# A decoder layer on one Trainium2 core: the last 6 feature blocks of the down projection as 7 products of quarters, placed at the end

## The chip, the core and the metric

The kernel runs on one core of a Trainium2 chip. The core has engines with instruction streams of their own: PE (TensorE, matrix products, with PEld for its weight loads), DVE (VectorE), ACT (ScalarE), POOL (GpSimd) and SP (SyncE, which here only issues transfers). They meet through semaphores. Transfers run on 16 DMA engines; SP, ACT and POOL issue them, and those that add to what lies at their destination are issued by POOL, on a software queue. The metric is the device time of one execution in microseconds: 1019.4 us, the median of three runs (1019.25 to 1019.58).

## The reference, cut to what matters

One layer (`DEPTH = 1`) on x of 512 positions by 1024 features, float32: a gated mixer of three branches, a residual sum, and a gated ConvFFN; at the end an RMSNorm. The part at issue is the last lines:

```python
def conv_ffn(u, w_up, conv_w, conv_b, w_down):
    h = causal_dwconv(u @ w_up, conv_w, conv_b)
    a, v = h[..., :D_FF], h[..., D_FF:]
    return (jax.nn.silu(a) * v) @ w_down          # D_FF = 2816, to 1024 features
...
        x = x + conv_ffn(rmsnorm(x, ln2_g[i]), ...)
    return rmsnorm(x, final_g)
```

## The kernel before

**Products.** Every float32 operand is split into a high and a low part (float32r): ACT casts the high part (`cast`, line 195, tile `wh` for weights), DVE subtracts it to get the low part (`lows`, line 217, tile `wl`; "the split" below), and `mm3` (line 230) issues high x high, high x low, low x high into one PSUM bank. So a product over n blocks of 128 features is 3n matmuls of 128x128 by 512 columns.

**Jobs.** The program is a list of `Job`s: a weight tile, and a body that issues the products with it. The loop at the end of `trunk` runs `prepare` and then the body of each: `prepare` of job n splits the weights of job n + 1 on DVE (and runs that job's `then`, if it has one), casts those of job n + 2 on ACT and fetches those of job n + 3 by SP (`fetch`, line 182) into one of two `raw` buffers. A job with `form` takes its weights from elsewhere than a fetch of its own, one with `load` set fetches nothing; one with `once` has the cast of job n + 2 issued whole in `prepare`, in two halves, otherwise a half at each `step`. `step()` is called between the products of a body and moves small sequences of other work on ("running"). PE, ACT, DVE and POOL execute their instructions in the order in which this program writes them down. A "read" below is DVE adding a finished bank to the residual `X1[tb, h]` (tb: 128 positions, four of them; h: half of the 1024 output features).

**The feed-forward part.** Of the 44 blocks of the up projection, 22 are gates and 22 values; `up_jobs` makes 22 jobs of two blocks. `up_evac` (line 1437) applies the convolution, and for a value block POOL multiplies it with its gate (line 1447); `later` then makes the operands of the down projection. The down projection runs over 22 feature blocks. The first 16 are two groups of 8 (`down_group`), each as 2x2 blocks of quarters in seven products in place of eight (the Strassen-Winograd scheme): positions are halved (`LO`, `HI`), features are halved into even and odd blocks, output features are halved. Their jobs are `one`, `five`, `three`, `six`, `seventh`, `two`, `four`, sums of the operands come from `sums_of` (four DVE operations of 256 columns, two casts, two splits for a pair of blocks), sums of weights from DVE (`diff`, line 343). The table `AT` says after which up job each of these jobs stands; the last two, `two` and `four`, stand after up job 21 and after the first job of the plain ending.

**The plain ending.** Blocks 16 to 21 go through `down_jobs(0)` and `down_jobs(1)`, one for each half of the output features: in each, a job of four blocks and one of two, and in them for each of the four tb a product over the blocks in their own operands (`ACTS`). In `down_jobs(1)` both jobs' products are held together (`tail=2`), so that it finishes one tb after another, 18 matmuls each. After the read of half 0 `early` (line 1586) takes the sum of squares and POOL multiplies by the gain (line 464); after the read of half 1 `norm_late` takes the other sum of squares on ACT (line 439), a square root on ACT (line 473), a reciprocal and its correction on DVE (lines 481 to 483), scales one half on DVE and one on ACT, and SP and ACT write both halves out (line 1605).

**A twin of the new ending.** The output projection of the mixer, `wo_group` (line 1266), is already a group of seven products over 8 blocks in the order `two, five, three, one, six, seven, four`, with a norm behind its last products (`first`, `then`), weight sums by adding transfers (`plus`, line 1288) and reads of two products replaced by a copy on ACT and an adding transfer of x (lines 1350 and 1351).

Of the kernel before, what the change touches and what calls it, by code (L numbers as in the profile page):

```python
# [10 lines left out]
F32 = mybir.dt.float32  # L11
# [5 lines left out]
P = 128  # L17
# [65 lines left out]
def trunk(ctx: ExitStack, tc, out, x, rel_bias, ln1_g, w_in, b_gate, w_a, pool_w, pool_scale, w_b,  # L83
# [22 lines left out]
    def T(name, dt=F32, shape=(P, S)):  # L106
        return big.tile(list(shape), dt, name=name, tag="t")
# [7 lines left out]
    def small(name, shape, dt=F32):  # L115
        return tiny.tile(list(shape), dt, name=name, tag="tiny")
# [110 lines left out]
    def wsrc(w, k0, k1, c0, c1):  # L227
        return w[k0 * P:k1 * P, c0:c1].rearrange("(k p) c -> p k c", p=P)
# [207 lines left out]
    def squares(eng, src, ss):  # L436
        junk = T("junk")
        if eng is act:
            act.activation(junk, src, AF.Square, accum_out=ss)
        else:  # L440
            dve.scalar_tensor_tensor(junk, src, 1.0, src, OP.mult, OP.mult, accum_out=ss)
# [14 lines left out]
            act.copy(hh, pv)  # L456
            dve.tensor_sub(ul[:, 4 * h:4 * h + 4, tb * P:(tb + 1) * P], pv, hh.bitcast(F32))

    def norm_early(t, g, h=0):

        ss, v0, xg = small("ss", [P, 1]), cpool.tile([P, 1], F32, name=f"v0_{len(V0)}"), T("xg")
        squares(act, t, ss)
        dve.tensor_scalar(v0, ss, 1.0 / D, EPS, OP.mult, OP.add)
        pool.tensor_tensor(xg, t, g[h], OP.mult)
        V0.append(v0)
        return v0, xg

    def norm_late(t, g, v0, outs, last, h=1, apart=False):


# [19 lines left out]
        (o1, x1), (o0, x0) = outs(xg)  # L490
        act.mul(o0, x0, rt)
        dve.tensor_scalar(o1, x1, rt, None, OP.mult)

    V0 = []

    uh = upool.tile([P, KD, S], F32R, name="uh", tag="uh")
    ul = upool.tile([P, KD, S], F32R, name="ul", tag="ul")
# [761 lines left out]
    def load_x1():  # L1259
        nxt["g2"] = grow(ln2_g[0])  # L1260
        act.activation(small("sq", [P, 1]), eps, AF.Sqrt)
        for tb, h in ((0, 1), (1, 1), (2, 0), (3, 0)):
            t = X1[tb, h] = T("x1")
            sp.dma_start(t, x[tb * P:(tb + 1) * P, h * S:(h + 1) * S])

    def wo_group():

        quarter = lambda two, h: w_o[:, h * S:(h + 1) * S].rearrange(
# [24 lines left out]

        def first(tb, h):
            half = 1 - h
            ss, xg = cpool.tile([P, 1], F32, name=f"so{tb}"), T("xg")
            squares(act, X1[tb, half], ss)
            pool.tensor_tensor(xg, X1[tb, half], nxt["g2"][half], OP.mult)
            nxt[tb] = ss, xg

        def then(tb, h):
            if "uh" not in nxt:
                nxt["uh"] = upool.tile([P, KD, S], F32R, name="uh2", tag="uh")
                nxt["ul"] = upool.tile([P, KD, S], F32R, name="ul2", tag="ul")
            ss, xg0 = nxt[tb]
            v0, vh = (cpool.tile([P, 1], F32, name=f"{n}{tb}") for n in ("va", "vo"))
            dve.tensor_scalar(v0, ss, 1.0 / D, EPS, OP.mult, OP.add)
            dve.tensor_scalar(vh, v0, -0.5, None, OP.mult)
            us = [T("u0"), T("u1")]
            it = norm_late(X1[tb, h], nxt["g2"], v0,  # L1310
                           lambda: (us[h], (us[1 - h], xg0)), vh, h, True)
            next(it)

            def rest(n=1):
                next(it, None)
                for _ in range(n):
                    yield
                norm_turn(us, nxt["uh"], nxt["ul"], tb)
# [118 lines left out]
    def up_evac(m, ps):  # L1437
        t = HC[m] = T("hc")
        act.activation(t, ps, AF.Identity, bias=ff["c1"][:, ff["b"] + m:ff["b"] + m + 1], scale=fw(2, m))  # L1439
        for k in range(2):  # L1440
            sh = 2 - k
            dve.scalar_tensor_tensor(t[:, sh:], ps[:, :S - sh], fw(k, m), t[:, sh:], OP.mult, OP.add)  # L1442
        if m < KF:
            act.activation(t, t, AF.Silu)  # L1444
            return
        a = HC[m - KF]
        pool.tensor_tensor(a, a, t, OP.mult)  # L1447

        def later():
            yield  # L1450
            k = m - KF
            if k >= KS or k % 2:
                h, l = T("fh", F32R), T("fl", F32R)
                act.copy(h, a)
                it = iter(())
                if k < KS:
                    it = sums_of(HC[k - 1], a, T("sah", F32R), T("sal", F32R),
                                 lambda j, h, l: FS.__setitem__((j, k // 2), (h, l)))
                    next(it)
# [123 lines left out]

    fin = {}

    def early(tb):
        yield
        v0, xg = norm_early(X1[tb, 0], fin["g"])
        vh = cpool.tile([P, 1], F32, name=f"vh{tb}")
        dve.tensor_scalar(vh, v0, -0.5, None, OP.mult)  # L1590
        fin[tb] = v0, vh, xg

    def down_jobs(h):

        def evac(tb, ps):
            t = X1[tb, h]
            dve.tensor_tensor(t, t, ps, OP.add)
            if h == 0:
                running.append(early(tb))
                return  # L1600
            v0, vh, xg0 = fin[tb]
            for _ in norm_late(t, fin["g"], v0, lambda xg1: ((xg1, xg1), (xg0, xg0)), vh):
                xg1 = _
            for i, o in ((1, xg1), (0, xg0)):
                (sp if i or tb < 3 else act).dma_start(out[tb * P:(tb + 1) * P, i * S:(i + 1) * S], o)

        return jobs_b(lambda k0, k1: [wsrc(w_down, KS + k0, KS + k1, h * S, h * S + S)], S,
                      lambda k, tb: ACTS[KS + k][0][:, tb * P:(tb + 1) * P],
                      lambda k, tb: ACTS[KS + k][1][:, tb * P:(tb + 1) * P], KF - KS, evac,
                      mk=(MM, SM)[h], tail=2 if h else 0)  # L1610


    class Call:
# [3 lines left out]
    def program():  # L1617
# [63 lines left out]
        between = {}  # L1681
        for group, ats in zip(groups, AT):
            for jobs_, at in zip(group, ats):
                between.setdefault(at, []).extend(jobs_)
        for i, job in enumerate(up_jobs()):
            yield job
            for load, ats in zip(loads, AT):
                if i == ats[0] - 3:
                    yield Call(load)
            yield from between.get(i, ())  # L1690
        yield Call(lambda: fin.setdefault("g", grow(final_g)))
        plain = down_jobs(0)
        yield next(plain)
        yield from between.get(2 * (KF // 2), ())
        yield from plain
        yield from down_jobs(1)

    jobs = list(program())
    weights = [j for j in jobs if isinstance(j, Job)]
# [216 lines left out]
```

## Time and profile before

| | |
|---|---|
| median of 3 runs | 1019.4 us |
| the profiled execution: its time | 1019.97 us |
| its span, first to last instruction | 1018.2 us |
| mean granted PE clock | 0.998 |
| DMA moved | 121.26 MB, mean 119 GB/s |
| software queue (POOL's transfers) | 2880 packets, 4.72 MB, 2.8% of the 16 engines' span |

In the rows below a timeline line reads: start in us from the span's start, duration in us, engine, source line, operation, tile written <- tiles read, shapes, count; in brackets the idle time before it on its engine and what released it. The chain of waits is followed back from the last instruction. Tiles: `pd` banks of the two groups, `pb` banks of the plain ending and of the output projection, `pu` of the up projection, `x` the residual, `wh`/`wl` high and low weights. The row of PE over a window gives us, PE busy (count), PEld, DVE, ACT and POOL busy, the clock, the DMA engines' share and GB/s.

### The profile page before, as it was taken

The page shows a single profiled execution, that of the slowest core. Times are in us where ns is not written, and L with a number is a line of the kernel's source. Part 1 is how long each engine was busy: PE and PEld are TensorE (multiplying, and loading weights), DVE is VectorE, ACT ScalarE, POOL GpSimd, SP SyncE. Part 2 cuts the span into 40 slices and gives each one's busy share as a digit, 9 for nine tenths or more (in the row PEclk, how much of TensorE's full clock was granted, in tenths as well). Part 3 has the DMA queues.
Part 4 walks back from the last instruction along what each step waited for, and adds up shares of the span by engine and source line. Part 5 has one row for each costly group of instructions (what it writes and reads, how often), then busy time and mean ns, then how long its engine had stood idle before and what let it go on. Part 6 is the DMA issues. An engine that isn't in the chain of part 4 may idle for free.

```text
span 1018.2 us, 13635 instructions
## 1 busy us (share of the span) xinstructions
PE 1005.1 (99%) x5378; PEld 856.6 (84%) x5378; DVE 718.1 (71%) x910; ACT 518.4 (51%) x878; POOL 147.7 (15%) x128
## 2 busy tenths in 40 slices
PE   8999999999999999999999999999999999999997
PEld 8898878999988888888888887898888888888885
DVE  6564768577767646676889688758778768685756
ACT  5433556454435565878567245554445444433434
POOL 1691000010000000000054501302111100111002
PEclk9999999999999999999999999999999999999999
DMA  8538222155254344552257346432322322321332
GB/s 265 174 99 213 86 81 76 47 159 154 89 182 118 101 121 108 145 136 79 76 160 183 124 143 161 133 125 84 111 96 83 112 94 85 123 83 42 124 104 83
DMA packets 114623, 121.26 MB, mean 119 GB/s; under 512 B 6499, under 2 KB 96166, under 8 KB 114559
## 3 DMA queue, kind: packets, MB, share of 16 engines
q1 hardware_dynamic: 111087, 114.81, 36.4%
q0 software_dynamic: 2880, 4.72, 2.8%
q8 instruction: 42, 0.69, 0.3%
q10 hardware_dynamic: 592, 0.86, 0.2%
q14 instruction: 22, 0.18, 0.1%
HBM read 116.58 MB, written 3.00 MB: 117 GB/s over the span
## 4 chain that ended last, share of the span: by engine, by line
PE 96%; DVE 2%; DMA 1%; ACT 0%; issue 0%; ACTq 0%; DVEq 0%
PE pa L238 36%; PE pu L238 23%; PE pb L238 10%; PE pd L238 7%; PE pqk L238 6%; PE pq L238 3%; PE pa L1764 2%; PE ps L786 1%; PE ppw L238 1%; PE po L834 1%; PE pt L820 1%; PE py L1119 1%; PE pu L1547 1%; DMA xin<-in_x_dram 1%; DVE wl L217 1%; PE pyo L1126 1%
## 5 line engine op out<-in xcount | busy, mean ns | idle before, releaser
L217 DVE TENSOR_TENSOR wl<-raw,wh 128x2048 fp32r<-128x2048 f32 (+3 forms) x87 | 202.9, 2332 | 47.6 <-ACT wh L195 33.9
L195 ACT CAST wh<-raw 128x1024 fp32r<-128x1024 f32 (+4 forms) x171 | 171.6, 1020 | 64.0 <-DVE raw L361 17.8
L1442 DVE SCALAR_TENSOR_TENSOR hc<-pu,fcol,hc 128x510 f32<-128x510 f32 x88 | 65.9, 748 | 56.4 <-ACT hc L1439 54.8
L238 PE MATMUL pa<-uh,wh 128*128 128x512 f32 (+1 forms) x368 | 88.8, 381 | 0.0
L238 PE MATMUL pa<-ul,wh 128*128 128x512 f32 (+1 forms) x368 | 86.8, 375 | 0.0
L238 PE MATMUL pa<-uh,wl 128*128 128x512 f32 (+1 forms) x368 | 86.8, 375 | 0.0
L238 PE MATMUL pu<-uh,wh 128*128 128x512 f32 (+1 forms) x352 | 83.5, 379 | 0.0
L238 PE MATMUL pu<-uh,wl 128*128 128x512 f32 (+1 forms) x352 | 83.5, 379 | 0.0
L238 PE MATMUL pu<-ul,wh 128*128 128x512 f32 (+1 forms) x352 | 83.5, 379 | 0.0
L238 PEld LDWEIGHTS pa<-ul,wh 128*128 128x128 f32 x368 | 66.7, 188 | 12.6
L238 PEld LDWEIGHTS pa<-uh,wl 128*128 128x128 f32 x368 | 66.7, 188 | 12.5
L238 PEld LDWEIGHTS pa<-uh,wh 128*128 128x128 f32 x368 | 65.3, 189 | 11.8
L238 PEld LDWEIGHTS pu<-uh,wl 128*128 128x128 f32 x352 | 64.2, 188 | 12.4
L238 PEld LDWEIGHTS pu<-ul,wh 128*128 128x128 f32 x352 | 64.2, 188 | 12.4
L238 PEld LDWEIGHTS pu<-uh,wh 128*128 128x128 f32 x352 | 64.1, 188 | 12.4
L1447 POOL TENSOR_TENSOR hc<-hc 128x512 f32<-128x512 f32 x22 | 30.8, 1398 | 284.8 <-DVE hc L1442 252.1
L1439 ACT ACTIVATE hc<-pu,fcol,fcol 128x512 f32<-128x512 f32 x40 | 31.2, 779 | 79.0 <-PE pu L238 79.0
L217 DVE TENSOR_TENSOR wl<-w,wh 128x2048 fp32r<-128x2048 f32 (+1 forms) x22 | 47.3, 2148 | 10.1 <-issue 4.6
L808 ACT ACTIVATE sb<-sb,nmls 128x128 f32<-128x128 f32 (+1 forms) x72 | 30.0, 418 | 31.5 <-DVE nmls L805 20.8
L195 ACT CAST wh<-w 128x1024 fp32r<-128x1024 f32 (+1 forms) x44 | 41.0, 971 | 4.8 <-PE pb L238 2.4
L1102 POOL TENSOR_TENSOR st<-st,dts 128x512 f32<-128x512 f32 x4 | 4.2, 1050 | 225.6 <-ACT st L1110 163.5
L1444 ACT ACTIVATE hc<-hc 128x512 f32<-128x512 f32 x22 | 13.9, 632 | 39.9 <-DVE hc L1442 39.9
(429 smaller groups left out, 1950.8 us busy)
## 6 DMA issues: line engine op xcount, KB each, us to landing
raw<-in_w_in_dram SPq DMA_DIRECT2D x24, 1024.0 KB, 5.8
raw<-in_ffn_w_up_dram SPq DMA_DIRECT2D x22, 1024.0 KB, 5.1
raw<-in_ffn_w_down_dram SPq DMA_DIRECT2D x8, 1024.0 KB
raw<-in_w_in_dram SPq DMA_DIRECT2D x14, 512.0 KB, 5.4
raw<-in_w_in_dram SPq DMA_DIRECT2D x8, 768.0 KB
raw<-in_w_b_dram SPq DMA_DIRECT2D x4, 1024.0 KB
al<-ad SPq DMA_DIRECT2D x16, 256.0 KB, 6.7
raw<-in_w_c_dram SPq DMA_DIRECT2D x4, 1024.0 KB, 5.0
```

The source lines that it names most:

```text
L195: (other.tensor_copy if other and i else act.copy)(job.high[:, :, o], job.raw[:, :, o])
L217: (eng or dve).tensor_tensor(l[:, :, o], job.raw[:, :, o], h[:, :, o].bitcast(F32), OP.subtract)
L238: pe.matmul(ps, l, r, start=first and n == 0, stop=last and n == total - 1, skip_group_check=onto)
L786: pe.matmul(pss[i][:, o:o + w * P], q[r, n * P:(n + 1) * P], k[r, kb * P:(kb + w) * P], start=True, stop=True)
L808: act.activation(sb[:, off:off + w * P], sb[:, off:off + w * P], AF.Exp, bias=nm[:, n, h:h + 1], accum_out=ls[:, n, h:h + 1])
L820: pe.transpose(pt[:, o:o + P], sb[:, o:o + P], eye)
L834: pe.matmul(po[DH * hh:DH * hh + DH, n * P:(n + 1) * P], V[g, kb + i][:, (2 * c + hh) * DH:(2 * c + hh + 1) * DH], probs[2 * c + hh, nb][: ...
L1439: act.activation(t, ps, AF.Identity, bias=ff["c1"][:, ff["b"] + m:ff["b"] + m + 1], scale=fw(2, m))
L1442: dve.scalar_tensor_tensor(t[:, sh:], ps[:, :S - sh], fw(k, m), t[:, sh:], OP.mult, OP.add)
L1444: act.activation(t, t, AF.Silu)
L1447: pool.tensor_tensor(a, a, t, OP.mult)
L1764: pe.matmul(first[2 * n + j][:, lo:hi], a[:, k, j * P:(j + 1) * P], b[:, k, lo:hi], start=a is wh and b is uh and k == 0, stop=a is wl and ...
```

## The change

The plain ending is replaced by a third group, `last_group`, of seven products over blocks 16 to 21 (three pairs), in the order `two, five, three, one, six, seven, four`, each product of 18 matmuls: two banks of 9. It stands behind both remaining jobs of group 2, which now both follow up job 21. For it `later` makes the sums of operands for the last three pairs as well. Three weight tiles hold W[0], W[1], W[2]: SP loads a quarter (`load`), and POOL's adding transfers, three of 256 KB for a quarter (`plus`), add others to it; `W[1]` gets its quarter added after `three`'s split (`three.then`). DVE makes one sum (`total`, in `one_read`). The products of `two` and `five` reach the residual by a copy on ACT and an adding transfer (`side_add`). Behind `one` and `seven` the sums of squares of the half just finished are taken (`first`), behind `six` (tb 0 and 1) and `four` (tb 2 and 3) the norm is finished and written out (`then`); for tb below 3 in the form that multiplies by scale and gain at once (`apart`). The gains are loaded, and the square root's table is called for, right after up job 21 (`begin`).

```diff
-    def norm_early(t, g, h=0):
...
+    COLS = [[cpool.tile([P, 1], F32, name=f"{n}{tb}") for n in ("so", "va", "vo")] for tb in range(4)]
...
         def later():
             yield
             k = m - KF
-            if k >= KS or k % 2:
+            if k % 2:
                 h, l = T("fh", F32R), T("fl", F32R)
                 act.copy(h, a)
-                it = iter(())
-                if k < KS:
-                    it = sums_of(HC[k - 1], a, T("sah", F32R), T("sal", F32R),
-                                 lambda j, h, l: FS.__setitem__((j, k // 2), (h, l)))
-                    next(it)
+                it = sums_of(HC[k - 1], a, T("sah", F32R), T("sal", F32R),
+                             lambda j, h, l: FS.__setitem__((j, k // 2), (h, l)), k >= KS)
+                next(it)
...
-    def early(tb):
...
-    def down_jobs(h):
...
+    def last_group():
+        n = (KF - KS) // 2
+        quarter = lambda two, h: w_down[KS * P:, h * S:(h + 1) * S].rearrange(
+            "(k two p) c -> two p k c", two=2, p=P)[two]
+        pairs = range(KS // 2, KF // 2)
+        W, A, B = {}, [], []
+        def side(j):
+            if j == "A11":
+                return [FS[0, p] for p in pairs]
+            if j in ("A12", "A22"):
+                half = LO if j == "A12" else HI
+                return [[t[:, half] for t in ACTS[2 * p + 1]] for p in pairs]
+            return [FS[j, p] for p in pairs]
+        def load(i, two):
+            W[i] = ypool.tile([P, 4, S], F32, name="w3", tag="xs")[:, :n, :]
+            sp.dma_start(W[i], quarter(two, 1))
+        def plus(i, two, h):
+            for k in range(n):
+                pool.dma_start(W[i][:, k, :], quarter(two, h)[:, k, :], accum_op=OP.add)
+        def begin():
+            fin["g"] = grow(final_g)
+            act.activation(small("sq", [P, 1]), eps, AF.Sqrt)
+        def first(tb, h):
+            half = 1 - h
+            ss, xg = COLS[tb][0], T("xg")
+            squares(act, X1[tb, half], ss)
+            pool.tensor_tensor(xg, X1[tb, half], fin["g"][half], OP.mult)
+            fin[tb] = ss, xg
+        def then(tb, h):
+            ss, xg0 = fin[tb]
+            _, v0, vh = COLS[tb]
+            dve.tensor_scalar(v0, ss, 1.0 / D, EPS, OP.mult, OP.add)
+            dve.tensor_scalar(vh, v0, -0.5, None, OP.mult)
+            o = {1 - h: xg0}
+            if tb < 3:
+                o[h] = T("xg")
+                it = norm_late(X1[tb, h], fin["g"], v0, lambda: (o[h], (xg0, xg0)), vh, h, True)
+                next(it)
+            else:
+                it = norm_late(X1[tb, h], fin["g"], v0, lambda xg: ((xg, xg), (xg0, xg0)), vh, h)
+                o[h] = next(it)
+            def rest():
+                next(it, None)
+                for i in (h, 1 - h):
+                    (sp if i == h or tb < 3 else act).dma_start(
+                        out[tb * P:(tb + 1) * P, i * S:(i + 1) * S], o[i])
+                yield
+            if tb < 2:
+                running.append(rest() if tb else after(1, rest()))
+            else:
+                for _ in rest():
+                    pass
+        def job(j, raw, form, bank, outs, more=False, op=OP.add, behind=None, side_add=False):
+            hi, h = outs
+            def body(ws):
+                wh, wl = ws
+                if not more:
+                    bank[:] = [MM("pb") for _ in range(2)]
+                parts = side(j)
+                for i in range(2):
+                    o = slice(i * P, (i + 1) * P)
+                    mm3(bank[i], lambda k: wh[:, k, :], lambda k: wl[:, k, :],
+                        lambda k: parts[k][0][:, o], lambda k: parts[k][1][:, o], range(n),
+                        flip=True, onto=more)
+                    tb = 2 * hi + i
+                    t = X1[tb, h]
+                    if side_add:
+                        r = T("r7")
+                        act.copy(r, bank[i])
+                        pool.dma_start(t, r, accum_op=OP.add)
+                    else:
+                        dve.tensor_tensor(t, t, bank[i], op)
+                    if behind:
+                        behind(tb, h)
+                    step()
+            new = Job([raw] if raw is not None else [], n, S, body)
+            new.form, new.once = form, True
+            if raw is None:
+                new.load = lambda: None
+            return new
+        def total(out, a, b, op=OP.add):
+            dve.tensor_tensor(out, a, b, op)
+            return out
+        def one_read(tb, h):
+            if tb == 0:
+                total(four.raw, four.raw, W[2])
+            first(tb, 1)
+        two = job("A12", quarter(1, 0), None, B, (0, 0), side_add=True)
+        five = job(1, None, lambda: W[0], B, (1, 1), side_add=True)
+        three = job(4, None, lambda: W[1], B, (0, 1), more=True)
+        one = job("A11", quarter(0, 0), None, A, (0, 0), behind=one_read)
+        six = job(2, None, lambda: W[2], A, (0, 1), more=True, op=OP.subtract, behind=then)
+        seven = job(3, None, lambda: W[1], A, (1, 1), more=True, op=OP.subtract,
+                    behind=lambda tb, h: first(tb, 0))
+        four = job("A22", quarter(1, 0), None, A, (1, 0), more=True, behind=then)
+        three.then = lambda: plus(1, 0, 1)
+        def soon():
+            four.load = None
+            fetch(four)
+            four.load = lambda: None
+        six.load = soon
+        return load, plus, begin, [two, five, three, one, six, seven, four]
...
         between = {}
         for group, ats in zip(groups, AT):
             for jobs_, at in zip(group, ats):
-                between.setdefault(at, []).extend(jobs_)
+                between.setdefault(min(at, 2 * (KF // 2) - 1), []).extend(jobs_)
+        load3, plus3, begin, group = last_group()
+        last = 2 * (KF // 2) - 1
+        extra = {16: [lambda: load3(0, 0)], 17: [lambda: plus3(0, 0, 0)], 19: [lambda: load3(2, 1)],
+                 20: [lambda: plus3(2, 0, 1)],
+                 last: [lambda: load3(1, 1), lambda: plus3(2, 0, 0), begin]}
         for i, job in enumerate(up_jobs()):
             yield job
             for load, ats in zip(loads, AT):
                 if i == ats[0] - 3:
                     yield Call(load)
+            for what in extra.get(i, ()):
+                yield Call(what)
             yield from between.get(i, ())
-        yield Call(lambda: fin.setdefault("g", grow(final_g)))
-        plain = down_jobs(0)
-        yield next(plain)
-        yield from between.get(2 * (KF // 2), ())
-        yield from plain
-        yield from down_jobs(1)
+        for job in group:
+            yield job
     jobs = list(program())
     weights = [j for j in jobs if isinstance(j, Job)]
```

More of the change, by code (lines that the diff above doesn't have):

```diff
@@ L457, in norm_turn @@
             dve.tensor_sub(ul[:, 4 * h:4 * h + 4, tb * P:(tb + 1) * P], pv, hh.bitcast(F32))
-    def norm_early(t, g, h=0):
[L461 to L466, printed above, removed]
     def norm_late(t, g, v0, outs, last, h=1, apart=False):
@@ L492, in norm_late @@
         dve.tensor_scalar(o1, x1, rt, None, OP.mult)
-    V0 = []
     uh = upool.tile([P, KD, S], F32R, name="uh", tag="uh")
@@ L1295, in first @@
             half = 1 - h
-            ss, xg = cpool.tile([P, 1], F32, name=f"so{tb}"), T("xg")
+            ss, xg = COLS[tb][0], T("xg")
             squares(act, X1[tb, half], ss)
@@ L1305, in then @@
             ss, xg0 = nxt[tb]
-            v0, vh = (cpool.tile([P, 1], F32, name=f"{n}{tb}") for n in ("va", "vo"))
+            _, v0, vh = COLS[tb]
             dve.tensor_scalar(v0, ss, 1.0 / D, EPS, OP.mult, OP.add)
@@ L1584, in trunk @@
     fin = {}
-    def early(tb):
[L1587 to L1591, printed above, removed]
-    def down_jobs(h):
[L1595 to L1610, printed above, removed]
+    def last_group():
[22 more added lines that the diff above has]
+            half = 1 - h
+            ss, xg = COLS[tb][0], T("xg")
+            squares(act, X1[tb, half], ss)
[3 more added lines that the diff above has]
+            ss, xg0 = fin[tb]
+            _, v0, vh = COLS[tb]
+            dve.tensor_scalar(v0, ss, 1.0 / D, EPS, OP.mult, OP.add)
[69 more added lines that the diff above has]
+        return load, plus, begin, [two, five, three, one, six, seven, four]
```

## Prediction

> **What bounds the kernel now.** I read the page first, then the chain of waits, then PE's share over the long stretch before the end.
>
> ```profile
> span 1018.2 us, 13635 instructions
> ...
> PE 1005.1 (99%) x5378; PEld 856.6 (84%) x5378; DVE 718.1 (71%) x910; ACT 518.4 (51%) x878; POOL 147.7 (15%) x128
> ```
>
> ```profile
> 673.00:1011.00 338.00, 338.00 (x1540) 282.02 (x1540) 243.27 (x266) 147.22 (x202) 36.78 (x26) 1.00 0.28 94
> ```
>
> From 673 to 1011 PE (the second number) has no gap, at clock 1.00, with DVE at 72% and the DMA engines at 28%. So a product taken out here shortens the run by its own slots as long as PE stays fed. The end of the chain of waits (start, us, what):
>
> ```profile
> 968.01 5.44 PE pd L238 x24
> 973.45 10.88 PE pb L238 x48
> 984.33 5.44 PE pd L238 x24
> 989.77 21.77 PE pb L238 x96
> ```
>
> One matmul takes 21.77 / 96 = 0.2268 us. The `pb` rows are the 144 matmuls that the change replaces; the last ends at 989.77 + 21.77 = 1011.54. After it comes the tail, read on DVE:
>
> ```profile
> 1011.57 0.69 DVE L1597 TENSOR_TENSOR x<-x,pb 128x512 f32<-128x512 f32 x1 [0.42 <-PE pb L238]
> ...
> 1013.37 0.16 DVE L481 RECIPROCAL r<-sq 128x1 f32<-128x1 f32 x1 [0.17 <-ACT sq L473]
> ```
>
> From the start of the last read of a bank to the end of the span: 1018.2 - 1011.57 = 6.63 us.
>
> **The change part by part.** *Removed:* 144 matmuls become 7 x 18 = 126, which saves 18 x 0.2268 = 4.08 us of PE. If PE is never held, group 2's last two products take 968.01 to 978.89, and the new ones end at 982.97 (`two`), 987.05 (`five`), 991.14 (`three`), 995.22 (`one`), 999.30 (`six`), 1003.38 (`seven`) and 1007.47 (`four`).
>
> *The pace.* A job is now 4.08 us and asks DVE for a weight split of 128x1536 (line 217), which stands in DVE's order ahead of the job's reads. The old ending split its last weights early and then ran 21.77 us without one. Prices of 1536 columns lie between these rows and two of the next fence (2048 columns in 2.28 on DVE, two halves in 1.98 on ACT):
>
> ```profile
> 984.42 1.23 DVE L217 TENSOR_TENSOR wl<-raw,wh 128x1024 fp32r<-128x1024 f32 x1 [6.12 <-PE pb L238]
> ...
> 989.59 1.14 ACT L195 CAST wh<-raw 128x512 fp32r<-128x512 f32 x2 [3.78 <-DMA raw<-in_ffn_w_down_dram]
> ```
>
> A split is (1.23 + 2.28) / 2 = 1.76 us, 1.68 from start to next start (the rows overlap by 0.08); a cast in two halves (1.14 + 1.98) / 2 = 1.56.
>
> *The six, seven, four stage.* The trace already holds this shape once: the output projection ends with the same three jobs, the same reads and a norm behind each. DVE there, then two rows of ACT:
>
> ```profile
> 640.22 2.42 DVE L217 TENSOR_TENSOR wl<-w,wh 128x2048 fp32r<-128x2048 f32 x1
> 642.55 0.68 DVE L1355 TENSOR_TENSOR x<-x,pb 128x512 f32<-128x512 f32 x1
> ...
> 644.02 0.16 DVE L478 SCALAR_TENSOR_TENSOR v<-ss,vo 128x1 f32<-128x1 f32 x1 [0.54 <-ACT junk L439]
> 645.05 0.69 DVE L1355 TENSOR_TENSOR x<-x,pb 128x512 f32<-128x512 f32 x1 [0.87 <-PE pb L238]
> ...
> 646.61 0.16 DVE L481 RECIPROCAL r<-sq 128x1 f32<-128x1 f32 x1
> ...
> 647.25 0.75 DVE L487 SCALAR_TENSOR_TENSOR u<-x,rt,grow 128x512 f32<-128x512 f32 x1
> ...
> 649.23 2.28 DVE L217 TENSOR_TENSOR wl<-raw,wh 128x2048 fp32r<-128x2048 f32 x1
> 651.43 0.68 DVE L1355 TENSOR_TENSOR x<-x,pb 128x512 f32<-128x512 f32 x1
> ```
>
> ```profile
> 643.26 0.63 ACT L439 ACTIVATE junk<-x 128x512 f32<-128x512 f32 x1 [0.31 <-DVE x L1355]
> ...
> 649.24 1.98 ACT L195 CAST wh<-raw 128x1024 fp32r<-128x1024 f32 x2
> ```
>
> DVE works through six's second read, the two norms (both `u`), four's split, and only then seven's first read. Seven's first read is what lets `four` overwrite that bank. From 645.05 to the read at 651.43 are 6.38 us; with 1.76 for 2.28 it is 5.86, and the read itself takes 0.68. PE needs only seven's 4.08 us in that time, so PE must wait. How late DVE enters decides by how much:
>
> - three's second product ends at 991.14: read 991.17, six's split 991.77 to 993.45, one's first read at 993.45 (a read is 0.68, 0.60 to the next start by the same overlap), the new sum `four.raw += W[2]` (1.68, priced as a split) to 995.73, one's second read to 996.33, seven's split to 998.0.
> - That split meets POOL's `xg` multiplication, which starts after one's first read. The row for such a meeting, a split of 2048 columns that began 0.36 us after a POOL multiplication:
>
> ```profile
> 970.57 1.59 POOL L1447 TENSOR_TENSOR hc<-hc 128x512 f32<-128x512 f32 x1 [3.55 <-DVE hc L1442]
> 970.93 3.38 DVE L217 TENSOR_TENSOR wl<-raw,wh 128x2048 fp32r<-128x2048 f32 x1
> ```
>
> It took 3.38 instead of 2.28, so 1.1 is the upper bound; the split at 640.22, also beside an `xg`, took 2.42, so 0.14 is the lower. I take 0.3, nearer to the same place in the twin stage: six's first read at 998.3. The Trainium skill (SBUF — State Buffer, section "Who interferes with whom") has a DVE instruction with two SBUF inputs blocked fully until such a GpSimd instruction is over; by that rule the split would wait for the rest of the POOL row, and the read would come at about 998.9, 0.6 later; the 3.38 row agrees with it.
>
> - ACT by then: square of one's second block (0.8 from 996.45; 643.26 to 644.02 in the rows, and a handoff), four's cast (1.56), free at 998.8, just in time. `v` follows the read by 644.02 - 642.55 = 1.47, so six's second read starts at 998.3 + 1.47 + 0.16 = 999.93, though PE had ended that product at 999.30.
> - Seven's first read: 999.93 + 5.86 = 1005.79, done 1006.47. `four` was due at 1003.38: PE waits **3.1 us**, with bounds 2.4 (no meeting, ACT on time, entry at PE's own 999.33) and 3.9 (meeting at 1.1).
>
> *The tail.* four's first product ends at 1006.5 + 2.04 = 1008.54, its second at 1010.58. Between the two DVE has a whole norm: 1.80 from read to reciprocal (tail rows), 0.64 to `u` (646.61 to 647.25), 0.67 for that (0.75 less the overlap), 3.1 in all, so the last read starts at 1011.67, **1.06 us** after its product. In the old ending 4.08 us lay between two reads, so no read stood behind a norm. From there 6.63 and 0.1 for two tiny operations now in the chain: 1018.4. Some six handoffs of 0.02 to 0.05 us bring it to 1018.6.
>
> *The sum:* -4.08 + 3.1 + 1.06 + 0.1 + 0.2 = **+0.4 us**. The profiled execution took 1019.97 with its span of 1018.2; it lies 0.57 above the median of 1019.4. So 1018.6, 1020.4 for that execution, 1019.8 as a median.
>
> *Edits that I cost at nothing.* The three pairs' extra sums on DVE, which had 28% of its time free there:
>
> ```profile
> 619.66 0.42 DVE L328 TENSOR_TENSOR sa<-yo 128x256 f32<-128x256 f32 x1
> ```
>
> Four such and about 1.4 us of splits more a pair. For the last pair they fall after 970.93's split (free at 974.31): read 0.6, sums and split 2.1, read 0.6, two's split 1.68 gives 979.3, and PE wants it after six matmuls, at 978.89 + 1.36 = 980.25; five's split is done at 983.4 against 984.33. PE covers both, by 0.9 us each; DVE 1 us later would cost as much. The other adding transfers have time: the last ones, onto `W[2]`, are issued after the up projection (968.01) and cast behind five (987.05), 19 us later. POOL's gate multiplications now stand behind three issues at a time (2.7 us by the w_o row below), and what they make is wanted a group job later at the earliest. On SP, ten transfers of 768 KB take the place of 3.1 MB, 4.7 MB more over about 90 us, some 52 GB/s beside the 94 of the second fence; each quarter is fetched two or more jobs ahead of its cast, into a buffer whose last reader is the split of a job before. The square-root table, loaded earlier now, was not in the chain before either. `side_add` moves four reads from DVE to ACT (0.53 each, last fence below) and POOL's queue; the blocks are wanted again only at `one` and `seven`.
>
> *The adding transfers of `W[1]`* are the one unpriced wait: three.then issues three of 256 KB after three's split, seven's cast waits for all three on ACT, and behind it on ACT stand one's squares, four's cast and six's squares; DVE's split of seven waits as well, and six's reads behind it. Rows: POOL's issues for the output projection, their landings (w, 540 to 560), those of the four onto x (620 to 640), and ACT's copy of a bank:
>
> ```profile
> 542.83 2.68 POOL L1288 DMA_DIRECT2D w<-in_w_o_dram  x3
> 546.85 0.87 POOL L1288 DMA_DIRECT2D w<-in_w_o_dram  x1 [1.34 <-issue]
> ```
>
> ```profile
> DMA to landing us min/median/max: 3.7/7.5/9.0
> ```
>
> ```profile
> DMA to landing us min/median/max: 4.1/4.8/7.8
> ```
>
> ```profile
> 621.77 1.06 ACT L1350 COPY x<-pb 128x512 f32<-128x512 f32 x2
> ```
>
> Three issue at once and the fourth 4.0 us after the first, about when the first has landed (3.7): I read three in flight at most. In the new queue two's `side_add`s stand first, issued at about 981.5 and 983.6 (product, then copy); three's split ends at 985.1, so the first transfer goes then, the second when the first `side_add` has landed, the third when the second has. With 4.8 us each: 986.3, 988.4, all landed at **993.2**. Seven's cast (1.56) and one's first square (0.8) have to be done by 996.45, so landing up to 994.1 costs nothing. Lower bound, 3.7 each: 991.0. Upper, 7.5 each: 983.6 + 7.5 + 7.5 = 998.6, which is 4.5 late. I take 4.8, since the second and third run beside no large load, as onto x, and keep 0 and 4.5.
>
> **Rivals.** *DVE and ACT keep pace* (faster): `four` starts at 1003.38. Its last read, still behind one norm, starts at 1007.47 - 2.04 + 0.03 + 3.1 = 1008.56, and 6.73 later the span ends at 1015.3: 2.9 us less, 1016.5. For it: DVE was 28% idle. Against it: the order on DVE, and the twin stage, where PE's four started only after that read:
>
> ```profile
> 652.57 1.17 PE L238 MATMUL pb<-wh,mgh 128*128 128x512 f32 x4
> ```
>
> (read until 652.11, though transposes stand between there.) *The `W[1]` transfers land late* (slower): from 994.1 on every us goes through ACT's order into six's reads and the end. At one landing of 7.5 among the 4.8s (995.9) it is +1.8, 1021.6; at 998.6 it is +4.5, 1024.3. For it: medians of 7.5 in the w row; against it: the emptier DMA engines. *The sums hold PE at the start of the group* (slower): 0.9 us of cover gone and 1 to 2 more, 1020.8 to 1021.8, only if DVE comes 2 to 3 us later than worked out. That fewer products are issued than said can't be otherwise: the loops count 126.
>
> **How the numbers follow.** The trade of PE slots for DVE's queue (1019.0 to 1021.2) 0.48; transfers late 0.28 (1021.4 to 1024.3); pace kept 0.15 (1016 to 1017.3); the group held at its start, 0.09. A measurement tells from no change about 0.2%, 2.04 us. The first case lies inside it, as does half of the last; late transfers lie beyond it nearly all: faster 0.16, same 0.50, slower 0.34. The range 1016.6 to 1023.4 takes in most of the others; the likeliest one's own is 1019.0 to 1021.2.
>
> **What would show it.** PE: 126 `pb` matmuls after 978.9, no gap until about 1003, then one of some 3 us before `four`'s first matmul, released by DVE's read, not by a weight. DVE between six's second read and seven's first: two `u` and a split without idle time over 0.6. ACT: no wait of seven's cast on `w` beyond 994. The last read about 1 us behind its product. I am wrong if PE has no gap before `four`, or if ACT's longest wait there is for a DMA.

## The result, and the profile after

| kernel | median, us | runs, us | ratio to before, 95% interval |
|---|---|---|---|
| before | 1019.27 (12 runs) | 1019.07 to 1021.23 | |
| changed | 1021.60 (12 runs) | 1020.09 to 1023.22 | 1.0019 [1.0010, 1.0028] |

The change made the kernel 0.2% slower, some 2 us, at the edge of what a measurement can tell from no change, and it made its time spread: the kernel before stayed within 0.5 us in 11 of these 12 runs, the changed one varies by 3 us. The profiled execution took 1020.77 with a span of 1019.0.

The start of group 2's last products, behind the up projection, lies between 966.9 and 968.0 us in nine of the ten profiles of this document (the tenth, no_w1_add, is looked at below). So that what happens earlier does not count, spans are compared here from that point on. In the chain of waits of the changed kernel (start, us, what) that is

```profile
966.93 10.88 PE pd L238 x48
```

against 968.01 before. From there to the end of the span it is 1018.2 - 968.01 = 50.19 us before and 1019.0 - 966.93 = 52.07 after: **+1.88 us**, where the sum of the prediction said +0.4. PE in the changed kernel's timeline, from seven's last matmuls on:

```profile
1001.72 0.84 PE L238 MATMUL pb<-wl,sbh 128*128 128x512 f32 x3
1005.61 0.93 PE L238 MATMUL pb<-wh,fh 128*128 128x512 f32 x3 [3.05 <-DVE x L1656]
1006.38 1.12 PE L238 MATMUL pb<-wh,fl 128*128 128x512 f32 x3
1007.30 1.49 PE L238 MATMUL pb<-wl,fh 128*128 128x512 f32 x3
1008.58 1.49 PE L238 MATMUL pb<-wh,fh 128*128 128x512 f32 x3
1009.86 1.01 PE L238 MATMUL pb<-wh,fl 128*128 128x512 f32 x3
1010.71 0.84 PE L238 MATMUL pb<-wl,fh 128*128 128x512 f32 x3
```

The wait stands in the second line: 3.05 us before `four`, released by a read on DVE. Then look at the distance of the starts. Three matmuls take 0.68 us at full clock; here they take 0.77, 0.92, 1.28, 1.28, 0.85, and only the last line lasts what such a line lasts elsewhere (0.84). The 18 matmuls of `four` took 1010.71 + 0.68 - 1005.61 = 5.78 us instead of 4.08. The granted clock (the number before the DMA share) in three stretches of 3.41 us each:

```profile
1003.38:1006.79 3.41, 1.18 (x5) 1.03 (x6) 2.68 (x3) 1.29 (x4) 1.25 (x1) 1.00 0.66 245
1006.79:1010.20 3.41, 3.41 (x9) 2.69 (x9) 0.91 (x3) 0.64 (x3) 1.29 (x2) 0.50 0.00 0
1010.20:1013.61 3.41, 1.35 (x6) 0.75 (x4) 2.94 (x10) 2.01 (x7) 0.00 (x0) 1.00 0.19 70
```

PE ran at half its clock for 3.41 us, from 1.18 us behind `four`'s start on; in the 3.41 us before that, the gap had left it only 1.18 us of work. DVE in the same kernel, the stage that the prediction followed:

```profile
997.41 0.67 DVE L1656 TENSOR_TENSOR x<-x,pb 128x512 f32<-128x512 f32 x1
...
998.95 0.68 DVE L1656 TENSOR_TENSOR x<-x,pb 128x512 f32<-128x512 f32 x1
...
1001.14 0.75 DVE L478 SCALAR_TENSOR_TENSOR xg<-x,rt,grow 128x512 f32<-128x512 f32 x1
...
1002.45 0.75 DVE L478 SCALAR_TENSOR_TENSOR xg<-x,rt,grow 128x512 f32<-128x512 f32 x1
1003.12 1.75 DVE L217 TENSOR_TENSOR wl<-raw,wh 128x1536 fp32r<-128x1536 f32 x1
1004.78 1.28 DVE L1656 TENSOR_TENSOR x<-x,pb 128x512 f32<-128x512 f32 x2
1008.82 0.69 DVE L1656 TENSOR_TENSOR x<-x,pb 128x512 f32<-128x512 f32 x1 [2.76 <-PE pb L238]
...
1012.00 0.68 DVE L1656 TENSOR_TENSOR x<-x,pb 128x512 f32<-128x512 f32 x1
```

Six's two reads, the two scalings of the norms, four's split, seven's two reads without a pause between: seven's first product was finished long before, and its read came last. The two reads at the end are four's.

### The profile page after: what moved, and what is told of

Its sections match the earlier page's. It is cut to its first block, busy times and chain, and to the rows that moved or that the text cites. A ratio compares the mean times of both kernels' runs of the same rounds, so it can differ in the third digit from the quotient of the medians.

```text
span 1019.0 us, 13694 instructions
## 1 busy us (share of the span) xinstructions
PE 1004.1 (99%) x5360; PEld 855.0 (84%) x5360; DVE 730.4 (72%) x931; ACT 528.4 (52%) x895; POOL 164.2 (16%) x144
## 4 chain that ended last, share of the span: by engine, by line
PE 94%; DVE 4%; issue 1%; ACT 1%; DMA 1%; ACTq 0%; DVEq 0%
PE pa L238 36%; PE pu L238 22%; PE pb L238 8%; PE pd L238 7%; PE pqk L238 6%; PE pq L238 3%; PE pa L1849 2%; PE ps L775 1%; DVE wl L217 1%; PE ppw L238 1%; PE po L823 1%; PE pt L809 1%; PE py L1108 1%; PE pu L1536 1%; DMA xin<-in_x_dram 1%
## 5 line engine op out<-in xcount | busy, mean ns | idle before, releaser
L217 DVE TENSOR_TENSOR wl<-raw,wh 128x2048 fp32r<-128x2048 f32 (+3 forms) x86 | 200.5, 2332 | 43.9 <-ACT wh L195 33.9
L195 ACT CAST wh<-raw 128x1024 fp32r<-128x1024 f32 (+3 forms) x169 | 169.9, 1022 | 50.6 <-DVE raw L361 17.8
L217 DVE TENSOR_TENSOR wl<-w,wh 128x2048 fp32r<-128x2048 f32 (+1 forms) x26 | 54.8, 2107 | 10.2 <-issue 4.6
L195 ACT CAST wh<-w 128x1024 fp32r<-128x1024 f32 (+1 forms) x52 | 47.2, 950 | 9.1 <-DMA w<-in_ffn_w_down_dram 4.3
```

What stands on the lines that cost most here:

```text
L195: (other.tensor_copy if other and i else act.copy)(job.high[:, :, o], job.raw[:, :, o])
L217: (eng or dve).tensor_tensor(l[:, :, o], job.raw[:, :, o], h[:, :, o].bitcast(F32), OP.subtract)
```

## The experiments

Each kernel was timed beside the kernel before on the same chip; kernels in one table share its runs (median 1019.19 in the first, 1019.34 in the second).

| kernel | median, us | runs, us | ratio to before, 95% interval |
|---|---|---|---|
| keep_warm | 1020.19 | 1020.09 to 1020.59 | 1.0010 [1.0001, 1.0020] |
| norms_after | 1019.84 | 1019.31 to 1020.98 | 1.0006 [0.9997, 1.0015] |
| no_w1_add | 1021.55 | 1019.80 to 1023.90 | 1.0023 [1.0013, 1.0032] |
| norms_split | 1018.14 | 1017.49 to 1018.83 | 0.9987 [0.9979, 0.9996] |

| kernel | median, us | runs, us | ratio to before, 95% interval |
|---|---|---|---|
| one_input | 1017.27 | 1016.53 to 1018.86 | 0.9979 [0.9970, 0.9988] |
| one_input_late | 1017.17 | 1016.94 to 1019.92 | 0.9982 [0.9973, 0.9991] |
| half_warm | 1020.33 | 1019.72 to 1020.58 | 1.0009 [1.0000, 1.0018] |
| dve_reads | 1021.65 | 1020.07 to 1024.98 | 1.0026 [1.0017, 1.0035] |

### Is the gap the cause of the slow matmuls?

keep_warm lets PE multiply something idle while it waits:

```diff
                     step()
+                if j == 3:
+                    d = MM("warm")
+                    for _ in range(13):
+                        pe.matmul(d, ones, wh[:, 0, :], start=True, stop=True)
```

> The changed kernel with 13 idle matmuls (ones by a weight tile, into a free bank that nothing reads) behind seven, 13 x 0.2268 = 2.95 us, inside the gap that PE has before four; nothing else changes. Theory A (PE's clock falls because of the 3.1 us gap, and that is what the sum of the prediction lacked): four's 18 matmuls take 4.1 us instead of 5.8, granted clock 1.00 there, four still starts at the same read; the last read comes about 1.0 us earlier, median 1020.3 to 1020.7, and the spread of the runs (1020.1 to 1023.2) falls below 1 us. Theory B (the slow matmuls have another cause, and the gap alone is the loss): the same 5.8 us, 1021.6.

PE in keep_warm, the idle matmuls and `four`:

```profile
1002.83 3.19 PE L1663 MATMUL warm<-wh,ones 128*128 128x512 f32 x13
1006.03 0.93 PE L238 MATMUL pb<-wh,fh 128*128 128x512 f32 x3
1006.80 0.85 PE L238 MATMUL pb<-wh,fl 128*128 128x512 f32 x3
1007.49 0.86 PE L238 MATMUL pb<-wl,fh 128*128 128x512 f32 x3
1008.19 0.85 PE L238 MATMUL pb<-wh,fh 128*128 128x512 f32 x3
1008.88 0.84 PE L238 MATMUL pb<-wh,fl 128*128 128x512 f32 x3
1009.55 0.84 PE L238 MATMUL pb<-wl,fh 128*128 128x512 f32 x3
```

`four` starts as late as in the changed kernel, and its lines now follow each other every 0.68 to 0.77 us: 4.2 us in all. The median falls by 1.4 us, the spread from 3.1 us to 0.5; no_w1_add, which has the gap and stands in the same table, has 1021.55. The fastest four of the changed kernel's 12 runs (1020.09 to 1020.59, mean clock 0.998) lie exactly in keep_warm's range, and the others, with mean clocks from 0.994 to 0.997, above it. That fits a loss that changes from run to run and is sometimes none. Theory A holds, and B falls.

DVE's two reads of `four` in keep_warm, which are needed further down:

```profile
1008.39 0.69 DVE L1656 TENSOR_TENSOR x<-x,pb 128x512 f32<-128x512 f32 x1 [1.91 <-PE pb L238]
...
1011.57 0.68 DVE L1656 TENSOR_TENSOR x<-x,pb 128x512 f32<-128x512 f32 x1
```

half_warm has 7 idle matmuls in place of 13, and so leaves a shorter gap.

> The changed kernel with 7 idle matmuls behind seven in place of keep_warm's 13: 1.59 us busy, then a gap of about 1.5 us before four. Theory A, with the gap's length as what counts (a gap of 1.75 us elsewhere in the trace is followed by full speed): four at full clock, 1020.2 as in keep_warm, spread below 1 us. Rival (any gap costs clock): slow matmuls in most runs, 1021 or more.

```profile
1003.07 1.80 PE L1663 MATMUL warm<-wh,ones 128*128 128x512 f32 x7
1006.27 0.94 PE L238 MATMUL pb<-wh,fh 128*128 128x512 f32 x3 [1.40 <-DVE x L1656]
```

A gap of 1.40 us costs its own length and no clock in this profile, and by the times (1019.72 to 1020.58) in none of the 11 runs. So a wait of 3.05 us can cost clock and one of 1.40 at the same place did not. The expectation's other case, 1.75 us without a loss, does not hold in every run: no_w1_add below shows half clock behind it.

### Does DVE's order make the gap?

norms_after keeps every instruction and moves the end of the first two norms on DVE and ACT behind seven's reads:

```diff
-                running.append(rest() if tb else after(1, rest()))
+                fin.setdefault("held", []).append(rest())
...
+        def then_held(tb, h):
+            first(tb, 0)
+            if tb == 3:
+                for it in fin["held"]:
+                    for _ in it:
+                        pass
...
-                    behind=lambda tb, h: first(tb, 0))
+                    behind=then_held)
```

> The changed kernel with the two norms behind six (reciprocal, correction, scaling: 2.6 us of DVE) written after seven's reads instead of before four's weight split. Theory A (DVE's order makes the gap, the gap the slow clock): four starts within 0.6 us of seven's end, its matmuls run at full clock; the two norms then delay four's first read by about 1 us; median about 1018 to 1018.8. Rival (the weights of four or ACT set four's start): a gap of 2 us or more stays, 1021 or more.

The gap before `four` in its timeline:

```profile
1003.79 0.93 PE L238 MATMUL pb<-wh,fh 128*128 128x512 f32 x3 [0.43 <-DVE x L1663]
```

From 3.05 to 0.43 us by order alone, and full clock behind it (the 18 matmuls take 4.20 us): DVE's order made the gap. ACT had finished the cast of four's weights at 997.5 in the changed kernel, long before. But the median was 1019.84, more than 1 us above what was expected. Where that went is in DVE's rows behind seven's reads:

```profile
1002.97 1.28 DVE L1663 TENSOR_TENSOR x<-x,pb 128x512 f32<-128x512 f32 x2
1004.35 0.69 DVE L473 SCALAR_TENSOR_TENSOR rt<-r,v 128x1 f32<-128x1 f32 x1
1005.08 1.22 DVE L474 SCALAR_TENSOR_TENSOR rt<-rt,r 128x1 f32<-128x1 f32 x1
```

and in POOL's beside them:

```profile
1003.73 2.56 POOL L1606 TENSOR_TENSOR xg<-x,grow 128x512 f32<-128x512 f32 x2 [4.29 <-DVE x L1663]
```

Two operations on one element a partition took 0.69 and 1.22 us, where they take 0.22 and 0.16 alone. The second ends at 1006.30, as POOL's second multiplication does (1003.73 + 2.56 = 1006.29).

norms_split also moves the 512-wide scaling of a block out of the chain, into the time in which DVE waits for ACT's squares of a later block (`scale` gives the factor at once, `late` scales); the last block is scaled in the same one operation, where the changed kernel multiplies by the gain first:

```diff
+            if tb > 1:
+                late(tb - 1)
+            t, o1 = X1[tb, h], T("xg")
...
+            fin["scale", tb], fin["end", tb] = scale, end
+            if tb > 1:
+                scale()
+            if tb > 2:
+                late(tb)
...
+            if tb == 3:
+                fin["scale", 0]()
+                late(0)
+                fin["scale", 1]()
```

> As norms_after, and the scaling that needs no early answer (one multiplication of 0.75 us a block of positions) is moved into the time in which DVE waits for ACT's squares of the next block; the last block is scaled in the same one operation. Theory A with the prediction's term for the tail (the last read stands 1 us behind its product because of the norm ahead of it): another 0.8 to 1.5 us less than norms_after, median 1016.5 to 1017.3, under the kernel before. If that term is wrong: no more than 0.3 us less than norms_after.

It is 1.70 us faster than norms_after and, at 0.9987, faster than the kernel before. Four's two reads in norms_after, then in norms_split:

```profile
1008.32 0.68 DVE L1663 TENSOR_TENSOR x<-x,pb 128x512 f32<-128x512 f32 x1
...
1011.43 0.68 DVE L1663 TENSOR_TENSOR x<-x,pb 128x512 f32<-128x512 f32 x1
```

```profile
1007.06 0.68 DVE L1670 TENSOR_TENSOR x<-x,pb 128x512 f32<-128x512 f32 x1
...
1009.46 0.68 DVE L1670 TENSOR_TENSOR x<-x,pb 128x512 f32<-128x512 f32 x1
```

From one read to the next it is 3.11 us in the first and 2.40 in the second, 0.71 less. From `four`'s start (1003.79 and 1003.33) to its first read it is 4.53 and 3.73, another 0.80 less. So the scalings cost at both places, and only the first of these gains lies between the two reads, where the prediction had its tail. The absolute value was missed by 0.8 us; the two slow operations of norms_after stand in norms_split's profile too (0.68 and 1.22 us).

### What held the tiny operations?

one_input writes these two operations with one tensor and scalars in place of two tensors:

```diff
-                dve.scalar_tensor_tensor(rt, r, v, r, OP.mult, OP.mult)
-                dve.scalar_tensor_tensor(rt, rt, 1.5, r, OP.add, OP.mult)
+                dve.tensor_scalar(rt, v, r, r, OP.mult, OP.mult)
+                dve.tensor_scalar(rt, rt, 1.5, r, OP.add, OP.mult)
```

> norms_split with the two correction operations of the scale (one element a partition, two tensors read from SBUF, 0.69 and 1.22 us there beside POOL's multiplications, 0.22 and 0.16 alone) written in the form that reads one tensor and two scalars; the arithmetic is the same. Theory C (DVE's operations with two SBUF inputs wait until POOL's multiplication is over, one with a single input does not): both take 0.15 to 0.25 us, four's first read comes about 1 us earlier, median 0.7 to 1.2 us under norms_split (1018.14), 1016.9 to 1017.4. Rival (these operations wait for something else, such as ACT's square root or the tile they write): unchanged times there and 1018.1.

DVE and POOL in one_input:

```profile
1004.06 0.27 DVE L1624 TENSOR_SCALAR rt<-v,r 128x1 f32<-128x1 f32 x1
1004.37 0.21 DVE L1625 TENSOR_SCALAR rt<-rt,r 128x1 f32<-128x1 f32 x1
1004.62 0.75 DVE L1631 SCALAR_TENSOR_TENSOR xg<-x,rt,grow 128x512 f32<-128x512 f32 x1
```

```profile
1003.43 3.10 POOL L1606 TENSOR_TENSOR xg<-x,grow 128x512 f32<-128x512 f32 x2 [4.29 <-DVE x L1670]
```

0.27 and 0.21 us beside a running POOL multiplication, and this time it was POOL's two that took longer, 3.10 instead of 2.56, beside DVE's scaling at 1004.62, which has two inputs. Theory C holds. The Trainium skill (SBUF — State Buffer, section "Who interferes with whom") gives the rule: a DVE instruction with two SBUF inputs and a GpSimd instruction that reads SBUF exclude each other for the whole instruction, and a DVE instruction with at most one SBUF input, outside its two-port modes, does not contend. These rows agree, down to one element a partition; the two scalars, which lie in SBUF as well, do not count as inputs in them. The median is 0.9 us under norms_split and 2.1 us under the kernel before in its own table.

one_input_late moves the scalings of the first two blocks behind four's reads, so that none meets POOL.

> one_input with the two 512-wide scalings of the first two blocks (0.75 us each, two SBUF inputs) moved behind four's first and second read, so that nothing with two inputs stands beside POOL's multiplications. Theory C: four's first read at once when its product ends; the moved scalings cost up to 0.5 us at the end; median 1016.6 to 1017.4, within 0.5 us of one_input. If the place of the scalings mattered more than the meeting with POOL, one of the two is 0.8 us or more ahead of the other.

1017.17 against 1017.27, with overlapping intervals: no difference that these runs can tell; the place of the scalings does not decide.

### Do the adding transfers matter?

no_w1_add leaves out the transfers onto `W[1]`:

```diff
-        three.then = lambda: plus(1, 0, 1)
```

> The changed kernel without the three transfers that add a quarter to W[1] behind three's split; product seven then lacks that quarter of the weights. Theory A: nothing on the path, the cast of seven comes 4 us earlier and has no effect: the gap before four stays at 3.0 to 3.3 us, median within 0.5 us of 1021.6. Rival (late adding transfers are the loss, at least in the slower runs): 1 us or more less, and a smaller spread.

1021.55 against 1021.60. In the changed kernel ACT waits long for these transfers, and it costs nothing:

```profile
992.33 1.57 ACT L195 CAST wh<-w 128x768 fp32r<-128x768 f32 x2 [4.27 <-DMA w<-in_ffn_w_down_dram]
993.81 0.63 ACT L439 ACTIVATE junk<-x 128x512 f32<-128x512 f32 x1
```

The cast ends in time for one's squares, and the split of seven begins only at 995.23. The spread of no_w1_add's runs (1019.80 to 1023.90) is no smaller than the changed kernel's. The slowest of them is the profiled one, and it lost clock at two places. The first lies ahead of everything that the change touches:

```profile
664.31 2.66 PE L1536 MATMUL pu<-uh,wl 128*128 128x256 f32 x16 [1.75 <-DVE wl L217]
```

```profile
662.33:665.74 3.41, 1.66 (x15) 1.43 (x13) 3.13 (x5) 2.61 (x4) 0.00 (x0) 1.00 0.10 10
665.74:669.15 3.41, 3.41 (x19) 3.41 (x18) 3.05 (x3) 0.82 (x2) 0.00 (x0) 0.50 0.86 297
```

All ten kernels have this wait (1.72 to 1.76 us; in the kernel before it ends at 664.78), and nine of their traces show full clock behind it. Here half clock follows, and group 2's last products start at 969.04. The second place is `four`:

```profile
1007.72 1.62 PE L238 MATMUL pb<-wh,fh 128*128 128x512 f32 x3 [3.02 <-DVE x L1656]
...
1014.10 0.86 PE L238 MATMUL pb<-wl,fh 128*128 128x512 f32 x3
```

```profile
1003.66:1007.07 3.41, 1.04 (x5) 0.54 (x3) 3.30 (x7) 1.09 (x2) 0.00 (x0) 1.00 0.65 241
1007.07:1013.90 6.83, 6.18 (x15) 4.86 (x16) 2.27 (x7) 2.35 (x7) 2.52 (x2) 0.50 0.09 33
```

Nearly the whole of `four` at half clock, 1014.10 + 0.68 - 1007.72 = 7.06 us instead of 4.08, behind a gap of the same 3.02 us. From 969.04 to the end of its span it is 53.06 us, against 51.24 in keep_warm: 1.8 us of this run's loss are `four`'s clock, and some 1.7 come from the first place.

While PE has work, half clock comes in these traces in stretches of 3.41 us or of twice that. In a stretch of 3.41 us at full clock just ahead of one, PE stood idle for 2.2 us (changed kernel), 2.0 (dve_reads) and 2.4 (`four` here), and for 1.75 at the first place. half_warm's 1.40 was followed by full clock, and so was keep_warm's 1.75 (at 664.13). So how a wait falls on such stretches seems to count beside its length; that this is why runs of one kernel differ was not tested, and each kernel has only one trace.

dve_reads undoes `side_add`:

```diff
-        two = job("A12", quarter(1, 0), None, B, (0, 0), side_add=True)
-        five = job(1, None, lambda: W[0], B, (1, 1), side_add=True)
+        two = job("A12", quarter(1, 0), None, B, (0, 0))
+        five = job(1, None, lambda: W[0], B, (1, 1))
```

> The changed kernel with the reads of two and five done by DVE, without the copies on ACT and the adding transfers onto the residual (side_add undone). The prediction costed side_add at nothing because DVE has time there: within 0.5 us of the changed kernel's 1021.6, with the same gap of 3.0 to 3.3 us before four; W[1]'s transfers land 1 to 2 us earlier because no other transfer stands before them, and nothing comes of it. Rival (side_add is what keeps DVE in time): 1 us or more slower, with PE waiting at five, three or one.

1021.65, with a gap of 3.03 us before `four`: the reads on DVE cost nothing there, as `side_add` gains nothing. One part of the expectation fell: with no other transfer ahead of them the three onto `W[1]` were issued at once, and the cast that needs them began at 993.15, not 1 to 2 us earlier than in the changed kernel but 0.8 later (both profiles reach group 2's last products at 966.9).

## Why the prediction was right, and the step that was not

Times from the start of group 2's last products, in us; what was predicted is reduced by 968.01, what was measured by 966.93.

| point | predicted | measured |
|---|---|---|
| six's first read | 30.29 | 30.48 |
| six's second read | 31.92 | 32.02 |
| seven's first read | 37.78 | 37.85 |
| `four` starts | 38.49 | 38.68 |
| four's first read | 40.56 | 41.89 |
| four's second read | 43.66 | 45.07 |
| end of the span | 50.59 | 52.07 |

- **Products saved.** 18 matmuls fewer (5360 in place of 5378), no gap up to seven: right.
- **The order on DVE, 3.1 us of waiting.** Right within 0.2 us at each of its points, because the twin stage of the same kernel had been timed row by row; norms_after shows that it was the order. In seven's split the meeting with POOL cost 0.5 (2.25 us instead of 1.75), where 0.3 was taken between 0.14 and 1.1.
- **Four's own matmuls.** The step that failed: "four's first product ends at 1006.5 + 2.04 = 1008.54" lets PE come back from a wait of 3 us at full clock. Its 18 matmuls took 5.78 us instead of 4.08. Of these 1.70 us 0.85 reach the end in the profiled execution (from four's start to its last read 6.39 us, in keep_warm 5.54), the rest is hidden behind the norm that stands between the two reads anyway. Over the runs the median lies 1.4 us above keep_warm's and the slowest run 3.0; how much of the slowest run's distance is `four`'s can't be told without its trace, as no_w1_add shows. The row that could have raised the question, a gap of 1.75 us without a slowdown in the kernel before, was shorter than this one. The Trainium skill (TensorE: Matmul & The Clock Gate, section "Why this matters for your kernels") asks for no idle gaps of PE over about 3 us, and says that one idle window of the activity monitor takes the clock to half; the traces agree for 3.05 and 3.02 us, which give 0.50, and for 1.40, which does not. They differ in that 1.75 us gave 0.50 too in no_w1_add, and in that the 3.41 us ahead of half clock were never wholly idle (1.18 us of work in the changed kernel). That page speaks against a gap like the one predicted, and the prediction did not weigh it.
- **The tail, 1.06 us.** Right: at full clock, in keep_warm, four's second product ends at 1009.55 + 0.68 = 1010.23 and its read starts at 1011.57, 1.34 later, where the first read stands 0.2 behind its product (1008.39 behind 1008.19); that is 1.1 us of waiting for the norm. norms_split takes 0.71 of the time between the two reads away. In the changed kernel itself only about 0.4 of it shows (the read at 1012.00, some 0.6 behind the product's end at 1011.39, where 0.2 is usual), since slow matmuls brought the second product late as well.
- **Handoffs and the end.** 0.2 us were taken for handoffs; from four's start to its last read keep_warm has 0.37 more than the prediction's 5.17, and from the last read to the end of the span it is 7.00 in the changed kernel and 7.03 in keep_warm, against 6.73. The 0.1 in these 6.73 for two more tiny operations was not there: from the last read to the issue of the last transfer it is 3.26 us in the kernel before and in the changed one. With 0.19 up to four's start, and the 0.2 of the sum taken off, that makes 0.6 us; so a kernel without loss of clock stands at +1.0, as keep_warm does. Why the span ends 0.37 us later behind that issue (3.74 against 3.37) stays open.
- **Edits at nothing.** Sums for three pairs, `side_add`, the transfers onto `W[1]`: each right. The transfers had landed by 992.33, that is 993.4 on the prediction's scale, against 993.2. In part that is luck: the last was issued at 986.57, 0.7 us earlier than worked out, and took some 5.6 us to land, where 4.8 was taken. The prediction's sign for being wrong, "if ACT's longest wait there is for a DMA", was badly put: that wait is there, 4.27 us, and no_w1_add shows that it costs nothing.
- **Rivals.** *DVE and ACT keep pace* and *the sums hold PE at the start of the group* did not come; *the W[1] transfers land late* would have given the measured time, and for another reason than the true one.

The forecast of no clear change held, and so did its range. But the measured 1021.6 lies above the range of the likeliest case alone, 1019.0 to 1021.2, and 1.4 us of the distance from 1019.8 is a mechanism that the sum did not have. That the wide range held is in part luck: its upper part was there for late transfers or a group held at its start, and neither came.

## What to carry to other kernels

When PE work is cut until another engine sets the pace, cost the wait twice: once for its length, and once for what PE's clock does behind it, which shows in the granted clock by stage and in the spread of the runs. A stage that exists once in a kernel is the best price list for its copy: DVE's order of six, seven and four was right to 0.2 us because it was read off there. What was needed was not fewer products but another order: with the norms' ends behind seven's reads, the wide scalings in DVE's waits and the small ones free of POOL, the same seven products end 2.1 us under the kernel before (one_input, 0.9979 [0.9970, 0.9988]).

## What the runs showed of the hardware that had not been expected

A wait of PE of 3.0 us was followed by half clock for 3.41 us in two traces and for 6.83 in a third, and the times say that some runs had none. A wait of 1.75 us was followed by 3.41 us of half clock in one trace of ten, and one of 1.40 us by none. And a DVE operation on one element a partition can last 1.22 us when it reads two tensors while POOL multiplies, 0.21 when it reads one.
